# Hybrid pooling and state-space layer on one core: split weights of z, z' and v kept in HBM, output weights prepared earlier, last z blocks between the first steps

## The chip, the core and the metric

The kernel runs on one core of a Trainium2 chip. The metric is the device time of one execution in microseconds (us); less is better. The core has five engines with queues of their own: TensorE (PE, with its weight loads as PEld), VectorE (DVE), ScalarE (ACT), GpSimd (POOL) and SyncE (SP, which here only starts DMA transfers). ACT starts transfers as well.

## The reference

One layer over 2048 latent tokens of width 1024 with a prefix of 256 context tokens. A normed and modulated input hm is projected to five parts: v (1024, for a pooling mixer), z' (its gate), z (the gate of the state-space mixer), x, B and C (2048 in all) and dt. The pooling mixer takes box means of v over windows 2, 4, 8, 16 on a 32 x 64 grid, less v itself, through a linear map for each group. The state-space mixer is a chunked scan in both directions, started from the context's final states. Both branches meet in one output projection.

```
hm = rmsnorm(h, norm_w) * (1 + scale) + shift;  p = hm @ w_in
y_pool = pool_mixer(v, pool_w, pool_scale) * silu(z')
y_s    = rmsnorm_by_group(ssd_bidir(conv(x, B, C), dt) * silu(z)) * ssd_norm_w
h      = h + g * (concat[y_pool, y_s] @ w_out);  out = rmsnorm(h, final_norm_w)
```

g comes, like scale and shift, from silu(c) @ w_ada + b_ada.

## The kernel before, in words

Products with weights are made in two parts: a weight or a token value is rounded to a high part, and the rest is kept as a low part; a product is hi x hi + hi x lo + lo x hi, three matrix products (project, from L227). The function weights (raw_weights L212 and split_weights) reads 0.5 MB of raw weights on SP's queue into one of two "wraw" buffers of rpool, lets ACT copy the high part (L219) and GpSimd subtract for the low part (L220), into one of two "w" buffers of wpool (1 MB each). All of it is one function, hybrid_block. Outside tc.manual_schedule() a planner orders the instructions of each engine, by written order and the times at which it expects operands; inside, they stand as written. The stages, with the times at which they run:

- **Start** (0 to 160). The linear map of the pool is multiplied into the weights of v (pool_map) and written to s_wp (map_store, L375, on SP). The modulation is made from w_ada. Tokens, one object for each block of 512 tokens, loads the tokens (x, xs, x2; L152), makes the norm (squares, mean, spread) and the modulated block hm[b] in a big buffer ("slot", of which there are four). Block b = 0 is modulated while the norms of blocks 1 and 2 are made; after each block come the columns 0 and 1 of x, B, C.
- **x, B, C stage** (160 to 492). The loop over columns ct from 2 to 15: 128 columns of weights each, read and split one column ahead; the context's product (ct under 12), four blocks of 512 tokens, the convolution on ACT and DVE (conv, L270), and writes to s_xt, s_bt and s_bc (conv_store, L258 on SP). At ct 10 to 13 gate_row reads eight rows of w_ada for g, through rpool; DVE sums them in gacc, which is written to s_gate.
- **Sweep stage** (492 to 823). For each of eight column groups j, the products of z, z' and v for the upper half of the tokens (blocks 2 and 3), with weights(...) for each. Between them runs sweep, the backward scan over 18 chunks and 4 groups: first makes split operands (bt, L641; xw, L644; xh, L649; xr, L651), second the states. At j = 1 the sum over partitions of gacc is multiplied into two PSUM banks gb, which stay held until the last rescale. From j = 2 on, eight blocks of w_out are read through rpool, scaled by rescale (L725, on DVE, from PSUM) and written to s_wo (unsplit).
- **Box stage** (823 to 1057). The lower half of the tokens (blocks 0 and 1): for each j of order the products of v and z' (box_pair) with box means on DVE, results in zt (one buffer), written to s_yp by ACT's queue after L828; with the first four, the z groups 0 to 3. following() hands out the weights and starts those of the next product. With the last four, prepare(0) to prepare(3). Then z groups 4 and 5, 1057 to 1079.
- **First steps** (1057 to 1150), written by hand in the string RAMP. 64 steps (chunk c, group g) make the forward scan, the gated norm and the output projection. Step.load starts six transfers on SP (L880 to L889): bc from s_bc (with silu of z), e1 and e2, tk, st. The chain of the norm is squares, square_sum, norm_mm, norm1, norm2, diag (L1014), spread. outputs is L973 and L979. Between the steps stand the z groups 6 and 7 (z makes the product, zg the silu and the write to s_bc) and the preparation of w_out: prep_load, prep_scale (k under 8), prep_hi, prep_lo, each through rpool, into four big buffers wout, each of which takes over the slot of a token block or a box buffer (more). prepare(9) to prepare(15) come after RAMP.
- **Steady steps** (1150 to 1681), all as written in ORDER.

## Time and profile before

| | us |
|---|---|
| median of 3 runs | 1691.6 |
| runs, lowest to highest | 1691.33 to 1699.04 |
| the profiled execution | 1691.25 |
| its span, first to last instruction | 1689.5 |
| PE busy in it | 1626.3 (96%) |
| DVE busy in it | 1209.4 (72%) |

The profile is of one execution. The page gives busy times by engine, the transfers, and the chain of work that ended last; views of the trace give the same by stretch of time (windows), by line and form of instruction, as a list in order of time (timeline), and as waits: an engine's idle time put down to the work that ended it. PEclk is TensorE's granted clock as a share of full speed (1.00 is 2.4 GHz, 0.50 is 1.2 GHz). A DMA share is the mean busy share of 16 DMA engines. Times within the execution count from the span's start.

### The profile page before, as it was taken

To read this page: it belongs to the slowest core of one execution; us is meant where nothing else is said; L and a number is where in the kernel's file an instruction comes from. 1 tells how busy PE (TensorE), PEld (TensorE's weight loads), DVE (VectorE), ACT (ScalarE), POOL (GpSimd) and SP (SyncE) were. 2 spreads that over 40 slices of the span, in tenths; PEclk is the share of its full clock that TensorE was granted. 3 is DMA by queue.
4 is the path that set the end of the run, shared out by engine and by line. 5 is a ranking of instruction groups with operands and counts; after the bars stand their busy time and mean duration, and the time that the engine had idled before them with its cause. 6 is when DMAs were issued, how large, how long until landed. Compare 5 with 4: busy or idle time off the path is not lost. (4 is left out here: it accounts for less than half of the span.)

```text
span 1689.5 us, 25001 instructions
## 1 busy us (share of the span) xinstructions
PE 1626.3 (96%) x7786; PEld 1306.6 (77%) x7786; DVE 1209.4 (72%) x2514; ACT 768.4 (45%) x1841; POOL 599.5 (35%) x667
## 2 busy tenths in 40 slices
PE   8889999999999999999999989869999999999997
PEld 6668888888887887787887868757888888888886
DVE  2575755566772888886199998547788888888885
ACT  5563453433453444443212122455565556555653
POOL 1231111111223667775433334323333333333331
PEclk9989999999999999999999999989999999999999
DMA  9823333466564678878624356675666667666762
GB/s 388 283 75 100 76 74 73 93 155 155 144 137 153 203 248 252 255 249 272 207 87 150 114 184 187 188 223 184 186 194 208 195 203 199 198 208 192 194 194 83
DMA packets 315543, 302.57 MB, mean 179 GB/s; under 512 B 132626, under 2 KB 244114, under 8 KB 312851
## 3 DMA queue, kind: packets, MB, share of 16 engines
q1 hardware_dynamic: 246594, 237.27, 48.9%
q10 hardware_dynamic: 68816, 63.71, 11.3%
q8 instruction: 61, 1.00, 0.2%
q14 instruction: 72, 0.58, 0.1%
HBM read 207.28 MB, written 93.62 MB: 178 GB/s over the span
## 5 line engine op out<-in xcount | busy, mean ns | idle before, releaser
L52 PE MATMUL px<-hm,w_x 128*128 128x512 f32 x1536 | 364.8, 397 | 2.7 <-ACT hm L205 2.4
L52 PEld LDWEIGHTS px<-hm,w_x 128*128 128x128 f32 x1536 | 288.0, 188 | 73.3 <-ACT hm L205 4.1
L52 PE MATMUL po<-wout,yp 128*128 128x512 f32 x768 | 213.0, 413 | 0.0
L52 PE MATMUL po<-wout,ys 128*128 128x512 f32 x768 | 211.0, 410 | 0.0
L52 PE MATMUL pz<-hm,w_z 128*128 128x512 f32 x768 | 188.9, 398 | 0.7 <-POOL w_z L220 0.7
L270 DVE SCALAR_TENSOR_TENSOR cacc<-u,conv_w,cacc 128x512 f32<-128x512 f32 x168 | 141.5, 854 | 66.3 <-POOL u L320 47.5
L52 PEld LDWEIGHTS pz<-hm,w_z 128*128 128x128 f32 x768 | 145.0, 189 | 36.0 <-POOL w_z L220 1.1
L52 PEld LDWEIGHTS po<-wout,yp 128*128 128x128 f32 x768 | 135.9, 190 | 34.7 <-issue 10.6
L52 PEld LDWEIGHTS po<-wout,ys 128*128 128x128 f32 x768 | 136.3, 190 | 23.7
L960 POOL TENSOR_TENSOR yp<-yl,yp 128x256 fp32r<-128x256 f32 x64 | 50.3, 786 | 229.2 <-ACT yp L956 220.8
L644 DVE TENSOR_TENSOR xw<-xt,w_t 128x256 f32<-128x256 f32 x144 | 99.3, 728 | 31.5 <-POOL xr L651 17.0
L651 POOL TENSOR_TENSOR xr<-xw,xh 128x512 fp32r<-128x512 f32 x72 | 99.7, 1387 | 27.4 <-ACT xh L649 27.4
L960 POOL TENSOR_TENSOR ys<-yg,ys 128x256 fp32r<-128x256 f32 x64 | 63.1, 986 | 116.9 <-ACT ys L956 66.6
L52 PE MATMUL ivationFunctionType.Copy<-hm,ivationFunctionType.Copy 128*128 128x512 f32 x384 | 97.7, 401 | 2.3 <-POOL ivationFunctionType.Copy L220 1.7
L52 PE MATMUL pv<-hm,w_v 128*128 128x512 f32 x384 | 92.9, 402 | 5.9 <-ACT zt L795 5.9
L52 PE MATMUL ivationFunctionType.Silu<-hm,ivationFunctionType.Silu 128*128 128x512 f32 x384 | 95.9, 396 | 0.0
L649 ACT CAST xh<-xw 128x512 fp32r<-128x512 f32 x72 | 44.7, 621 | 110.0 <-DVE xw L644 48.9
L52 PE MATMUL pzp<-hm,w_q 128*128 128x512 f32 x384 | 91.3, 396 | 1.2 <-ACT va L788 1.2
L52 PEld LDWEIGHTS pv<-hm,w_v 128*128 128x128 f32 x384 | 73.6, 192 | 24.1 <-ACT zt L795 6.3
L52 PEld LDWEIGHTS ivationFunctionType.Copy<-hm,ivationFunctionType.Copy 128*128 128x128 f32 x384 | 73.1, 191 | 20.5 <-POOL ivationFunctionType.Copy L220 2.1
L52 PEld LDWEIGHTS pzp<-hm,w_q 128*128 128x128 f32 x384 | 72.0, 188 | 19.2 <-ACT va L788 1.6
L904 ACT ACTIVATE e<-e,nrb_t 128x128 f32<-128x128 f32 x256 | 81.1, 388 | 12.2 <-DMA e<-s_rows 11.9
(269 smaller groups left out, 3046.3 us busy)
## 6 DMA issues: line engine op xcount, KB each, us to landing
e<-s_rows SPq DMA_DIRECT2D x128, 256.0 KB, 5.1
s_tok<-tkw ACTq DMA_DIRECT2D x64, 256.0 KB, 3.0
bc<-s_bc SPq DMA_DIRECT2D x64, 256.0 KB, 4.3
st<-s_tok SPq DMA_DIRECT2D x64, 256.0 KB, 5.5
xt<-s_xt SPq DMA_DIRECT2D x72, 128.0 KB, 3.4
ada<-in_w_ada_dram SPq DMA_DIRECT2D x8, 1024.0 KB, 15.7
wraw_x<-in_w_xbc_dram SPq DMA_DIRECT2D x16, 512.0 KB, 4.4
s_bc<-cacc ACTq DMA_DIRECT2D x32, 256.0 KB, 3.2
```

Source lines behind the costliest of these rows:

```text
L52: nc.tensor.matmul(o, l, r, start=start, stop=stop)
L270: nc.vector.scalar_tensor_tensor(acc, u[:, k:k + n], conv_w[:, ct, k:k + 1], acc, op0=ALU.mult, op1=ALU.add)
L644: nc.vector.tensor_tensor(xw[:, s], h4(xt), w_t[:, s, c, 4 * g:4 * g + 4].unsqueeze(2).broadcast_to([P, 4, 64]), op=ALU.mult)
L649: nc.scalar.copy(xh, xw)
L651: nc.gpsimd.tensor_tensor(xr, xw, xh.bitcast(F32), op=ALU.subtract)
L904: nc.scalar.activation(s.e2[:, h, :], s.e2[:, h, :], AF.Identity, bias=nrb_t[:, s.c, 4 * s.g + h:4 * s.g + h + 1])
L960: nc.gpsimd.tensor_tensor(y[:, 1], src, y[:, 0].bitcast(F32), op=ALU.subtract)
```

## The change

Weights of z, z' and v: the sweep stage splits each group once (kept_weights) and writes both parts, 1 MB, to s_w on SP's queue, each after the read of the next group's raw weights (save). The box stage and the first steps read them back as split tiles (saved_weights), with no work on ACT or GpSimd. rpool closes after the sweep stage.

Output weights: prep(k) reads, scales, splits and writes all 16 blocks of w_out to s_wo, in columns 8 to 11 of the x, B, C stage, four a column, through rpool and one "wo" buffer. prepare(k) becomes one read of 1 MB. For this the gate rows move from columns 10 to 13 to columns 3 to 6, their product goes through two aux PSUM tiles back into gacc in SBUF, and s_gate and the banks gb are gone. The raw weights of columns 3 to 15 are read on ACT's queue instead of SP's.

z groups 4 and 5 of the lower half move into RAMP, among the first steps, with groups 6 and 7; the function w there takes the next weights. prepare(4) to prepare(13) stand in RAMP as reads, prepare(14) and (15) behind it.

Start: the buffer of block 1 is taken right after its read; the writes to s_wp, x2 and the reads of blocks 2 and 3 move into the modulation of block 0, the writes inside a block that orders what it holds behind the last square of block 1. Smaller moves: rowscale and allone are made before the x, B, C stage, wd lies in another pool, kp opens ahead of RAMP.

```diff
     s_wp = dram("s_wp", [8, P, 8, P])
+    s_w = dram("s_w", [24, P, 2, 8, P])
...
-    s_gate = dram("s_gate", [P, 1024])
-    s_wo = dram("s_wo", [8, P, 1024])
+    s_wo = dram("s_wo", [16, P, 2, 1024])
...
+    wpool = wstack.enter_context(tc.tile_pool(name="wpool", bufs=2, side="right"))
     rpool = rstack.enter_context(tc.tile_pool(name="rawp", bufs=2, side="right"))
-    wpool = wstack.enter_context(tc.tile_pool(name="wpool", bufs=2, side="right"))
...
     latent(1, xs[:, 1])
-    x2 = slot("x2", [P, 2, 8, 512], F32)
-    latent(2, x2[:, 0])
-    latent(3)
-    for g in range(4):
-        map_store(g)
+    latent_slot(1)
...
     for b in range(4):
-        if b > 0:
+        if b > 1:
             latent_slot(b)
...
+            if (b, k) == (0, 1):
+
+                with tc.issue_after(tok[1].last.ins):
+                    for g in range(4):
+                        map_store(g)
+                x2 = slot("x2", [P, 2, 8, 512], F32)
+                latent(2, x2[:, 0])
+                latent(3)
...
-            nc.scalar.dma_start(s_gate, gacc)
+            for j in range(2):
+                gb = aux(f"gb{j}")
+                mm(gb, allone, gacc[:, 512 * j:512 * j + 512], True, True)
+                nc.scalar.copy(gacc[:, 512 * j:512 * j + 512], gb)
+
+    def prep(k):
+
+        raw = rpool.tile([P, 1024], F32, tag="wraw", name=f"wos{k}")
+        nc.sync.dma_start(raw, d["w_out"][k * P:(k + 1) * P, :])
+        for j in range(2):
+            js = slice(512 * j, 512 * j + 512)
+            nc.vector.scalar_tensor_tensor(raw[:, js], raw[:, js], rowscale[:, k:k + 1], gacc[:, js],
+                                           op0=ALU.mult, op1=ALU.mult)
+            w = gp.tile([P, 2, 512], F32R, tag="wo", bufs=1, name=f"wo{k}_{j}")
+            nc.scalar.copy(w[:, 0], raw[:, js])
+            nc.gpsimd.tensor_tensor(w[:, 1], raw[:, js], w[:, 0].bitcast(F32), op=ALU.subtract)
+            nc.sync.dma_start(s_wo[k, :, :, js], w.bitcast(F32))
...
         if ct < 15:
-            wx[ct + 1] = weights(d["w_xbc"][ct + 1], f"x{ct + 1}")
+            raw = rpool.tile([P, 8, P], F32, tag="wraw", name=f"wraw_x{ct + 1}")
+            nc.scalar.dma_start(raw, d["w_xbc"][ct + 1])
+            wx[ct + 1] = split_weights(raw, f"x{ct + 1}")
...
             col.conv()
+            if 8 <= ct < 12:
+                prep(4 * ct - 32 + b)
...
-        if ct in (10, 11, 12, 13):
+        if 3 <= ct < 7:
             for k in range(2):
-                gate_row(2 * ct - 20 + k)
+                gate_row(2 * ct - 6 + k)
...
-        def rescale(raw, k):
-
-            for j in range(2):
-                js = raw[:, 512 * j:512 * j + 512]
-                nc.vector.scalar_tensor_tensor(js, js, rowscale[:, k:k + 1], gb[j], op0=ALU.mult, op1=ALU.mult)
+        unsaved = []
+
+        def kept_weights(i, src, nm):
+
+            w = weights(src, nm)
+            save()
+            unsaved.append((i, w))
+            return w
+
+        def save():
+            for i, w in unsaved:
+                nc.sync.dma_start(s_w[i], w.bitcast(F32))
+            unsaved.clear()
...
-            w = weights(d["w_z"][j], f"z{j}_2")
+            w = kept_weights(j, d["w_z"][j], f"z{j}_2")
...
-            if j == 1:
-                gacc = rpool.tile([P, 1024], F32, tag="wraw", name="gacc2")
-                nc.sync.dma_start(gacc, s_gate)
-                gb = [pp(f"gb{j}") for j in range(2)]
-                for j in range(2):
-                    mm(gb[j], allone, gacc[:, 512 * j:512 * j + 512], True, True)
-            for k in {1: (), 7: (5, 6, 7)}.get(j, (j - 2,) if j else ()):
-                raw = rpool.tile([P, 1024], F32, tag="wraw", name=f"wos{k}")
-                nc.sync.dma_start(raw, d["w_out"][1024 + k * P:1152 + k * P, :])
-                rescale(raw, 8 + k)
-                nc.scalar.dma_start(s_wo[k], raw)
...
-                w = weights(src, f"p{j}_{fn}")
+                w = kept_weights((8 if fn == AF.Silu else 16) + j, src, f"p{j}_{fn}")
...
+        save()
+    rstack.close()
...
+    def saved_weights(i, nm):
+        w = wpool.tile([P, 2, 8, P], F32R, tag="w", name=f"w_{nm}")
+        nc.sync.dma_start(w.bitcast(F32), s_w[i])
+        return w
...
-            ahead.append(weights(*sources.pop(0)))
+            ahead.append(saved_weights(*sources.pop(0)))
...
     def prepare(k):
-        prep_load(k)
-        prep_scale(k)
-        prep_hi(k)
-        prep_lo(k)
+        nc.sync.dma_start(wout[k // 4][:, k % 4].bitcast(F32), s_wo[k])
...
-    for i in (4, 5):
-        w = following()
-        for b in lower:
-            z_block(ep, w, i, b)
-        if i == 4:
-            prepare(i)
     estack.close()
     yp_ = ctx.enter_context(tc.tile_pool(name="poolp", bufs=2))
-    ws = [following() for _ in range(2)]
+    ws = []
...
     def z(j, b):
-        zps[j, b] = z_product(ws[j - 6], j, b)
+        zps[j, b] = z_product(ws[j - 4], j, b)
...
+    def w():
+        ws.append(following())
+
+    kp = ctx.enter_context(tc.tile_pool(name="workp", bufs=2))
...
     RAMP = """
-    0:load prep_load/5 1:load 0:scores 0:carried 0:shift 0:mask 0:exponents prep_scale/5 1:shift 0:steps_mix
-    prep_hi/5 logs 0:decay z/6/0 1:scores 1:carried zg/6/0 z/7/0 0:mix 0:from_states prep_load/6 
...
+    0:load w z/4/0 1:load 0:scores 0:carried 0:shift 0:mask 0:exponents 0:steps_mix logs 0:decay
+    w z/5/0 0:mix 0:from_states 0:mix2 prepare/4 prepare/5 1:scores 1:carried 1:shift 1:mask 1:exponents 1:steps_mix
+    1:decay zg/4/0 zg/5/0 2:load 0:load_pool 0:outputs z/4/1 1:mix 1:from_states 1:mix2 0:gate logs 0:squares
+    0:square_sum 0:state 0:norm_mm 1:outputs 2:scores 2:shift 2:mask 2:exponents 2:steps_mix 2:decay z/5/1
+    0:norm1 1:gate 0:norm2/0 0:norm2/1 0:norm2/2 0:norm2/3 0:diag 1:squares 1:square_sum 1:load_pool prepare/6
+    prepare/7 0:spread 2:carried zg/4/1 zg/5/1 w 0:scale z/6/0 w 2:mix 2:from_states 2:mix2 logs 0:ssd_hi 0:ssd_lo
+    1:norm_mm 2:outputs 1:norm1 1:state 1:norm2/0 1:norm2/1 1:norm2/2 1:norm2/3 1:diag z/7/0 2:gate 2:squares
+    2:square_sum 1:spread zg/6/0 zg/7/0 more 3:load prepare/8 prepare/9 1:scale logs 0:pool_hi 0:pool_lo 1:ssd_hi
+    1:ssd_lo prepare/10 prepare/11 z/6/1 2:norm_mm 3:scores 3:carried 3:shift 3:mask 3:exponents 3:steps_mix 3:decay
...
     """
...
-    for k in range(9, 16):
+    for k in range(14, 16):
         prepare(k)
-    rstack.close()
+    wstack.close()
```

## Rows read from the trace of the kernel before

**Rows 1.** The page, busy time of each engine, its share of the span and instructions.

```profile
PE 1626.3 (96%) x7786; PEld 1306.6 (77%) x7786; DVE 1209.4 (72%) x2514; ACT 768.4 (45%) x1841; POOL 599.5 (35%) x667
```

**Rows 2.** Windows by stage: stretch, length, busy of PE PEld DVE ACT POOL, PEclk, DMA, GB/s.

```profile
0.00:160.00 160.00, 139.29 (x662) 107.12 (x663) 81.76 (x149) 83.56 (x170) 38.76 (x48) 0.95 0.62 221
160.00:492.00 332.00, 332.00 (x1532) 272.42 (x1531) 219.94 (x308) 146.35 (x224) 54.31 (x146) 1.00 0.51 110
492.00:823.00 331.00, 325.04 (x1372) 258.76 (x1371) 230.67 (x383) 136.19 (x295) 202.11 (x163) 0.99 0.72 229
823.00:1057.00 234.00, 226.95 (x963) 181.87 (x962) 196.40 (x72) 46.58 (x65) 85.57 (x54) 0.99 0.47 148
1057.00:1150.00 93.00, 72.43 (x326) 56.67 (x324) 51.99 (x108) 46.77 (x94) 31.35 (x22) 0.89 0.67 202
1150.00:1690.00 540.00, 530.63 (x2938) 429.71 (x2938) 428.65 (x1498) 308.92 (x996) 187.37 (x234) 1.00 0.64 188
```

**Rows 3.** Waits of PE: us in total, times, longest us.

```profile
PE n L52 <- ACT dg L1014: 8.9, 2, 4.9
...
PE yo L52 <- DMA st<-s_tok: 6.8, 1, 6.8
PE rstd_l L52 <- ACT dgl L134: 6.1, 2, 5.9
PE pv L52 <- ACT zt L795: 5.9, 1, 5.9
PE st L52 <- DVE bt L641: 3.4, 4, 1.8
```

**Rows 4.** Timeline of SP's queue, 45 to 62: start, us, what.

```profile
49.79 1.55 SPq L152 DMA_DIRECT2D x<-in_xT_dram  x1
...
56.13 5.56 SPq L152 DMA_DIRECT2D xs<-in_xT_dram  x1
```

**Rows 5.** Groups by line and form, L651 and L649: busy, mean ns.

```profile
L651 POOL TENSOR_TENSOR xr<-xw,xh 128x512 fp32r<-128x512 f32 x72 | 99.7, 1387 | 27.4 <-ACT xh L649 27.4
...
L649 ACT CAST xh<-xw 128x512 fp32r<-128x512 f32 x72 | 44.7, 621 | 110.0 <-DVE xw L644 48.9
```

**Rows 6.** Timelines of DVE (1078 to 1095) and of POOL (270 to 284).

```profile
1079.99 1.13 DVE L899 SCALAR_TENSOR_TENSOR e<-e,af_t,e 128x128 f32<-128x128 f32 x4
1081.38 1.41 DVE L725 SCALAR_TENSOR_TENSOR wor<-wor,rowscale,gb 128x512 f32<-128x512 f32 x2 [0.26 <-DMA wor<-in_w_out_dram]
1086.38 6.12 DVE L935 SCALAR_TENSOR_TENSOR m<-cbl,dt_t,m 128x128 f32<-128x128 f32 x4 [3.59 <-ACT m L927]
...
277.53 2.42 POOL L220 TENSOR_TENSOR w_x<-wraw_x,w_x 128x1024 fp32r<-128x1024 f32 x1 [0.77 <-ACT w_x L219]
```

**Rows 7.** DMA issues: count, KB each, median us from issue to landing.

```profile
wraw_x<-in_w_xbc_dram SPq DMA_DIRECT2D x16, 512.0 KB, 4.4
...
s_wo<-wos ACTq DMA_DIRECT2D x8, 512.0 KB, 3.2
```

**Rows 8.** Timeline of PE, columns 11 to 15 and both ends of the boxes.

```profile
379.66 112.15 PE L52 MATMUL px<-hm,w_x 128*128 128x512 f32 x480
...
823.11 11.36 PE L52 MATMUL pz<-hm,w_z 128*128 128x512 f32 x48
...
1056.77 22.56 PE L52 MATMUL pz<-hm,w_z 128*128 128x512 f32 x96
```

**Rows 9.** Timeline of SP's queue, 310 to 340.

```profile
318.97 15.00 SPq L258 DMA_DIRECT2D s_bt<-u  x12
```

**Rows 10.** A window of 10 us in the sweep stage, columns of rows 2.

```profile
700.00:710.00 10.00, 10.00 (x44) 8.08 (x44) 10.00 (x13) 3.84 (x12) 8.72 (x7) 1.00 0.80 261
```

**Rows 11.** The chain that ended last, 1040 to 1165: start, us, what.

```profile
1065.17 5.09 DMA s_yp<-zt
...
1071.24 7.30 DMA e<-s_rows
```

**Rows 12.** A window of 5 us in the first steps, columns of rows 2.

```profile
1125.00:1130.00 5.00, 3.16 (x17) 2.50 (x17) 2.82 (x7) 2.42 (x4) 0.00 (x0) 0.50 0.84 216
```

More of the change, by code (lines that the diff above doesn't have):

```diff
@@ L333, in hybrid_block @@
     dt_raw = const("dt_raw", [P, NC2, 32], pool=dp)
-    wd = dp.tile([P, 8, P], F32R, tag="wd", name="wd")
+    wd = sp.tile([P, 8, P], F32R, tag="wd", bufs=1, name="wd")
     ctxt = Tokens(hc, 256, d["ctxT"], 1, "c", wpool.tile([P, 8, 256], F32, tag="w", name="xc"))
@@ L763, in hybrid_block @@
         if i < 4:
-            sources.append((d["w_z"][i], f"z{i}"))
-        sources += [(s_wp[j], f"v{j}"), (d["w_zp"][j], f"q{j}")]
-    sources += [(d["w_z"][i], f"z{i}") for i in range(4, 8)]
-    ahead = [weights(*sources.pop(0))]
+            sources.append((i, f"z{i}"))
+        sources += [(16 + j, f"v{j}"), (8 + j, f"q{j}")]
+    sources += [(i, f"z{i}") for i in range(4, 8)]
+    def saved_weights(i, nm):
+        w = wpool.tile([P, 2, 8, P], F32R, tag="w", name=f"w_{nm}")
+        nc.sync.dma_start(w.bitcast(F32), s_w[i])
+        return w
+    ahead = [saved_weights(*sources.pop(0))]
     def following():
@@ L833, in hybrid_block @@
     wout = [slot("wout0", [P, 4, 2, 1024], F32R)]
-    raws = {}
-    def prep_load(k):
-        raws[k] = rpool.tile([P, 1024], F32, tag="wraw", name=f"wor{k}")
-        nc.sync.dma_start(raws[k], s_wo[k - 8] if k >= 8 else d["w_out"][k * P:(k + 1) * P, :])
-    def prep_scale(k):
-        if k < 8:
-            rescale(raws[k], k)
-    def prep_hi(k):
-        nc.scalar.copy(wout[k // 4][:, k % 4, 0, :], raws[k])
-    def prep_lo(k, eng=None):
-        wo = wout[k // 4][:, k % 4]
-        eng = eng or (nc.gpsimd if k in (1,3,4,5,7,13,15) else nc.vector)
-        eng.tensor_tensor(wo[:, 1, :], raws[k], wo[:, 0, :].bitcast(F32), op=ALU.subtract)
     def prepare(k):
-        prep_load(k)
-        prep_scale(k)
-        prep_hi(k)
-        prep_lo(k)
+        nc.sync.dma_start(wout[k // 4][:, k % 4].bitcast(F32), s_wo[k])
     with tc.tile_pool(name="boxp", bufs=1) as xp:
@@ L1203, in hybrid_block @@
-    other = {f.__name__: f for f in (prep_load, prep_scale, prep_hi, prep_lo, z, zg, logs, work, more)}
+    other = {f.__name__: f for f in (prepare, z, zg, logs, w, more)}
     RAMP = """
-    0:load prep_load/5 1:load 0:scores 0:carried 0:shift 0:mask 0:exponents prep_scale/5 1:shift 0:steps_mix
-    prep_hi/5 logs 0:decay z/6/0 1:scores 1:carried zg/6/0 z/7/0 0:mix 0:from_states prep_load/6
-    0:mix2 1:mask 1:exponents 2:load prep_scale/6 1:steps_mix prep_hi/6 1:decay zg/7/0 2:scores 2:carried more
@@ L1211, in hybrid_block @@
-    1:from_states 1:mix 0:outputs z/6/1 prep_lo/5 prep_load/7 0:load_pool prep_lo/6
-    0:gate 2:mask prep_scale/7 1:mix2 prep_load/8 1:load_pool 0:squares 2:shift
-    2:steps_mix 0:square_sum 2:exponents 1:outputs 0:norm_mm z/7/1 more work prep_hi/8 prep_hi/7 zg/6/1 prep_lo/8
-    0:state prep_lo/7 3:load 2:from_states 1:gate 0:pool_hi 1:squares zg/7/1 logs 0:norm1
-    1:square_sum 0:norm2/0 1:pool_hi 2:decay 2:mix 0:pool_lo 1:pool_lo 3:scores 1:norm_mm 0:out/0/0
-    0:out/0/1 1:norm1 0:norm2/1 0:norm2/2 0:norm2/3 0:diag 0:spread 2:mix2 3:mask 2:outputs 1:out/0/0 0:scale 3:carried 1:out/0/1
@@ L1219, in hybrid_block @@
+    2:norm1 2:state z/7/1 1:pool_hi 1:pool_lo zg/6/1 zg/7/1 more prepare/12 prepare/13 logs 2:norm2/0 2:norm2/1
+    2:norm2/2 2:norm2/3 0:out/0/0 0:out/0/1 1:out/0/0 1:out/0/1
     """
```

13 lines of the change are left out of this document (3 added, 10 removed).

## The prediction, made before the changed kernel was run

> **What bounds the kernel now.** I read the busy table first [rows 1]: TensorE is busy 1626.3 of 1689.5 us, so an edit can only win back TensorE's idle time, 63 us, and the time in which its clock is down. The profiled execution took 1691.25 us, 1.75 more than its span and 0.35 under the median of the three runs, 1691.6; the sum is made against 1691.25. Next I read the span by stage [rows 2], the stage's length less its PE column. The x, B, C stage (160 to 492) has no TensorE idle at all. The rest is 20.7 us in the start, 6.0 in the sweep stage (492 to 823), 7.1 in the box stage (823 to 1057), 20.6 in the first steps (1057 to 1150) and 9 in all that follows. The waits of TensorE [rows 3] name them: the spread of the second token block's norm in the start (6.1), the DVE's split bt in the sweep (3.4), ACT's silu into zt in the box stage (5.9), and in the first steps the chain of the step norm (8.9) and one load of st (6.8). About 0.5% (8.5 us) is what a measurement of this kernel can tell from no change.
>
> **The start.** The read of the third block (x) goes out before that of the second (xs), at 49.8 against 56.1, and writes of s_wp stand around both [rows 4]. After the change block 1 gets its own buffer without waiting for the s_wp writes, and x and s_wp come later. The read at 56.1 could then go out some 5 us earlier, behind the first row of writes instead of the second. What that buys is the wait for the spread, 6.1 us [rows 3], and perhaps 2 us of the clock behind it (the stage's mean is 0.95, [rows 2]); x, now late, is first needed after a whole block of products. I take -5, between 0 and -8. The block that ties the stores to an instruction of ACT holds only transfers that SP starts, so it may tie nothing; then only the written order acts, and I leave the 5.
>
> **The x, B, C stage.** Added: 16 preparations of output weights, each a read of 0.5 MB, two DVE scalings, two ACT copies, two GpSimd subtractions, two writes of 0.5 MB; and the two gate products, moved from the sweep, which are worth nothing in the sum. Of engine time there is enough: GpSimd is at 54.3 of 332 us and would add 32 x 1.39 = 44; ACT 146 + 32 x 0.62 = 166 [rows 2, 5]; DVE 220 + 32 x 0.7 = 243 [rows 2, 6]. DVE does lose time when GpSimd subtracts: four small operations that take 1.13 us in one row took 6.12 beside two subtractions [rows 6]; if all 44 us were lost so, DVE would stand at 287 of 332, still under. What is short is buffers. The split piece wo has one buffer, so a half goes copy 0.62, subtract 1.39, write 3.2 [rows 5, 7], then the next: 5.2 us, and 32 halves take 167. The preparations share the two raw buffers with the x weights, and behind the raw weights of a column that wait for their turn stands TensorE. In this sum I let the x weights, now read on ACT's own queue, get a buffer ahead of the preparations that were written earlier, so that the chain simply fills the time from column 8 to the stage's end, 191 us (column 8 begins at 301, three columns of 22.4 and 2.9 of context ahead of column 11, whose latent products begin at 379.7 [rows 8]), and I charge +4 for a late column, between 0 and the +44 of the first rival. The SP queue is crossed too: a row of twelve s_bt writes held it for 15 us [rows 9], and the s_wo writes go behind such a row.
>
> **The sweep.** Removed: 16 scalings on DVE (16 x 0.7 = 11 us; three blocks of weights stood at the end, where bt is waited for), eight reads and eight writes of 0.5 MB, and the two PSUM banks that the gate product held from here to the first steps. Added: 24 writes of 1 MB on SP. They wait for a split that has ended by then, because each is written behind the next weights' read; behind them on SP stand the sweep's reads of xt and bl and its writes of hb. Added less removed is 24 - 8 = 16 MB in 331 us, 48 GB/s. The stage runs at 229 GB/s and a share of 0.72 [rows 2]; at 0.80 it moved 261 [rows 10], so 277 would be a share of about 0.85: close, not full. I take -2 (of the 3.4 on bt), between -4 and +10 (a few reads of 3 to 5 us stuck behind writes). The Trainium skill, DMA: Bandwidth & Descriptors, section Bandwidth, gives 425 GB/s for a 16 MB transfer; by that figure an estimate of the stage would have a third to spare and no cost at all. The trace's share leaves less room than that.
>
> **The box stage.** Removed: 20 splits of weights on ACT and GpSimd and four preparations. Added: weight reads of 1 MB in place of 0.5, and only two weight tiles in place of two raw and two split ones; a read starts when the tile before last is free and then has a group's 11.2 us, against some 5, the 5.09 of a 1 MB write [rows 11]. Twenty groups of 11.2 us make 224 us, yet the stage takes 1056.77 - 823.11 = 233.7 [rows 8]: 9.7 us are lost, 5.9 of them through the full PSUM behind zt [rows 3], the rest in the clock after it and in a small wait. The two banks given back alone let TensorE run on for two blocks while silu waits, and DVE loses the 8 scalings and the collisions with GpSimd. I take -9, between 0 and -9.7.
>
> **The first steps.** Eight z blocks (8 x 5.6 = 45 us of products) now stand between the steps, four of them, 22.6 us, moved in from before [rows 8]. They can cover the norm's waits. Against this: the first load of a step came just behind the write of the last box result, a write of 5.09 us that ended at 1070.3; e of that load went out at 1071.2 [rows 11]. Those four blocks covered that wait; now one block of 5.6 does. The last box group would end at 1047; silu, one DVE product and the write bring the first load to about 1056, its scores to 1060, its states to 1064: TensorE idles some 9 us. Then 3 MB (z6 and two output tiles) stand on SP ahead of the third step's load, and the fourth load waits until z6 and z7 are written: 0 to 9 and 4 to 8 us. Lost before: 20.6 us idle and some 5 of half clock (0.50, TensorE's lower level of 1.2 GHz, in a stretch of this stage) [rows 2, 12]. Lost after: 9 + 3 + 5 and about 2 of clock, 19 in round numbers. I take -7; bounds -20 (nearly all gone) and +9 (every wait at its worst). The 12 preparations on ACT, DVE and GpSimd that go away free these engines, not TensorE.
>
> **The sum.** -5 + 4 - 2 - 9 - 7 = -19: 1691.25 - 19 = 1672.
>
> **Rivals.** First, slower: the raw buffers go out in written order. Column 13's weights are then behind preparation 15 and need what preparation 14 frees. The first preparation can begin when column 8's split ends at 280 [rows 6] plus a read of 4.4 [rows 7]; 29 halves of 5.2 later it is 435; then 2 to the end of its subtraction, 4.4 to read, and 3.6 to split the weights (2.42 for GpSimd's part and twice 0.62 for ACT's) [rows 5, 6]: 445. Column 13 begins at 379.7 + 2 x 22.4 = 424.5 (five columns in 112.15, [rows 8]). TensorE stands 21 us; with each write delayed by 0.8 on the SP queue (halves of 6.0) it is 44. At 35, and without the +4, the kernel takes 1691.25 - 23 + 35 = 1703. It decides from a half of about 4.5 us on. For it: the single wo buffer, and the measured 3.2 us of a write. Against it: the reads have moved to ACT's queue and stand in no row of SP's any more. The Trainium skill, DMA: Bandwidth & Descriptors, section Issuing engines are not separate DMA queues, says that starting transfers from several engines saves only the starter's time; by that rule the move shortens no read, and this rival's 1703 would come out. No row here shows a read of weights from ACT's queue.
>
> Second, no change: the first steps give back what the box stage won. The load that waits for the result, the third and the fourth load each at their upper bound make 9 + 9 + 8 us and the clock 4 after them, 30 in place of 26; with a sweep that gains nothing, because the writes fill its DMA engines, and a start whose order doesn't change: 1691.25 + 4 + 0 - 9 + 4 = about 1690. For it: the e of the first load took 7.3 us to land [rows 11]. Against it: eight blocks leave much to put between.
>
> Third, the change doesn't act at the start: -14 in place of -19, 1677, still faster, so it is inside the forecast's own range, 1657 to 1682.
>
> **How the numbers follow.** Forecast and its variants 0.47, first rival 0.31 (of it 0.27 beyond +0.5% and 0.04 within), second 0.18, and 0.04 for a loss through the sweep's writes that reaches the size of the first rival. So faster 0.47, same 0.04 + 0.18 = 0.22, slower 0.27 + 0.04 = 0.31. The range takes in the forecast's lower side (1657) and reaches into the first rival to 1709; what lies above (halves of 6 us and more) and below is under 2 in 10.
>
> **What would show it.** Right: no TensorE wait on the x weights between 400 and 470, a box stage of 225 us with no wait on zt, the norm's waits gone from the first steps, the first steps' loss under 20 us, a busy total still at 1626. Wrong: a wait of TensorE on ACT's or GpSimd's part of w_x of 10 us or more (first rival); waits on bc or st of 10 us and more after 1047 (second); DMA shares of 1.0 in the sweep with waits on bt or xr.

## The result, and the profile after

The changed kernel takes 1779.38 us (median of 4 runs, 1775.73 to 1780.92) where the kernel before took 1691.46 beside it: a ratio of 1.052, 95% interval 1.0494 to 1.0545. The forecast was 1672, with a range up to 1709. The profiled execution took 1775.73 us.

The page of the changed kernel, span and busy times (before: [rows 1]):

```profile
span 1773.8 us, 25046 instructions
PE 1638.1 (92%) x7786; PEld 1310.6 (74%) x7786; DVE 1159.6 (65%) x2505; ACT 754.8 (43%) x1839; POOL 540.9 (30%) x668
```

TensorE's work is what it was but for 12 us of slower clock, and its idle time went from 63 to 136 us. The same stages as in [rows 2], in windows of the changed kernel; the columns are those of [rows 2], the bounds are where the same products begin:

```profile
0.00:150.70 150.70, 129.40 (x624) 99.30 (x625) 73.21 (x138) 78.59 (x163) 38.55 (x47) 0.95 0.65 234
150.70:551.90 401.20, 349.58 (x1572) 285.11 (x1571) 244.92 (x343) 165.99 (x259) 97.49 (x177) 0.93 0.61 153
551.90:898.50 346.60, 328.20 (x1370) 256.95 (x1369) 228.98 (x374) 139.34 (x299) 200.64 (x164) 0.99 0.80 265
898.50:1124.70 226.20, 224.37 (x962) 180.39 (x961) 154.79 (x63) 23.80 (x40) 7.12 (x32) 1.00 0.61 206
1124.70:1245.00 120.30, 86.28 (x382) 67.51 (x382) 35.89 (x118) 43.71 (x101) 13.89 (x19) 0.83 0.71 247
```

The x, B, C stage, which had no idle at all, now has 51.6 us of it; the sweep 18; the boxes 2; the first steps 34. In the x, B, C stage the products also run 9 us longer than before, at a granted clock of 0.93 where it was 1.00. The waits of TensorE in the changed kernel say on what (before: [rows 3]):

```profile
PE px L52 <- ACT w_x L219: 42.9, 2, 22.0
PE yo L52 <- DMA st<-s_tok: 18.2, 3, 9.8
PE st L52 <- DVE bt L665: 15.4, 17, 2.3
PE cb L52 <- DMA bc<-s_bc: 14.5, 2, 9.2
PE pc L52 <- ACT w_x L219: 8.7, 1, 8.7
...
PE rstd_l L52 <- ACT dgl L134: 5.8, 1, 5.8
```

All runs are read by the same four lengths: when the first z product begins (the end of the x stage), the sweep (to the first z product of the lower half), the boxes (to the end of the last z' product) and the rest. Spans are of the profiled executions; ratios are to the kernel before on the same chip.

| run | first z at | sweep | boxes | rest | span | ratio (interval) |
|---|---|---|---|---|---|---|
| before | 491.7 | 331.5 | 233.8 | 632.6 | 1689.5 | 1 |
| after | 551.9 | 346.5 | 226.2 | 649.1 | 1773.8 | 1.052 (1.0494 to 1.0545) |
| e2_two_small | 533.9 | 344.9 | 226.6 | 650.2 | 1755.6 | 1.0407 (1.0386 to 1.0428) |
| e3_x_on_sp | 545.0 | 340.9 | 226.5 | 649.5 | 1761.9 | 1.0466 (1.0436 to 1.0496) |
| e4_spread | 510.9 | 354.1 | 226.2 | 647.5 | 1738.6 | 1.0297 (1.0275 to 1.0318) |
| e5_few_saves | 552.8 | 324.4 | 226.6 | 649.8 | 1753.6 | 1.039 (1.0371 to 1.0408) |
| e6_saves_act | 551.9 | 336.3 | 228.1 | 647.9 | 1764.3 | 1.0451 (1.0413 to 1.0488) |
| e7_old_ramp | 552.2 | 345.2 | 226.3 | 626.3 | 1750.0 | 1.0384 (1.0347 to 1.0422) |
| e8_load_first | 552.6 | 345.8 | 226.6 | 648.5 | 1773.5 | 1.0505 (1.0472 to 1.0537) |
| e9_one_prep | 494.1 | 345.1 | 228.2 | 649.9 | 1717.3 | 1.0145 (1.0106 to 1.0184) |
| e10_no_keep | 494.9 | 318.4 | 226.3 | 633.6 | 1673.1 | 0.9899 (0.9884 to 0.9914) |
| e11_all_mended | 503.3 | 348.1 | 226.6 | 631.5 | 1709.5 | 1.0148 (1.0126 to 1.017) |
| e12_hold_banks | 494.6 | 318.4 | 226.5 | 632.8 | 1672.3 | 0.99 (0.9873 to 0.9927) |
| e13_keep_alone | 493.7 | 349.8 | 224.2 | 625.7 | 1693.3 | 1.0027 (1.001 to 1.0043) |
| e14_hold_longer | 494.0 | 318.4 | 232.6 | 627.5 | 1672.5 | 0.9912 (0.9896 to 0.9929) |
| e15_keep_four | 493.7 | 318.9 | 229.9 | 627.0 | 1669.5 | 0.989 (0.9875 to 0.9905) |

From before to after the span grew by 84.3: the start -0.6, the x stage +60.9, the sweep +15.1, the boxes -7.6, the rest +16.5.

### The profile page after: what moved, and what is told of

It is laid out like the page before. It is cut to its first block, busy times and chain, and to the rows that moved or that the text cites. A ratio compares the mean times of both kernels' runs of the same rounds, so it can differ in the third digit from the quotient of the medians.

```text
span 1773.8 us, 25046 instructions
## 1 busy us (share of the span) xinstructions
PE 1638.1 (92%) x7786; PEld 1310.6 (74%) x7786; DVE 1159.6 (65%) x2505; ACT 754.8 (43%) x1839; POOL 540.9 (30%) x668
## 4 chain that ended last, share of the span: by engine, by line
PE 51%; DMA 15%; DVE 5%; issue 3%; POOL 2%; SPq 1%; ACT 1%; ACTq 0%; DVEq 0%; POOLq 0%
PE po L52 21%; PE pz L52 6%; PE pzp L52 5%; PE pv L52 4%; DMA s_wo<-wo 3%; DMA xt<-s_xt 3%; PE yo L52 3%; PE y L981 2%; PE ivationFunctionType.Silu L52 2%; PE y L987 2%; PE ivationFunctionType.Copy L52 2%; DMA s_tok<-hb 2%; DVE xw L668 2%; DVE cacc L270 1%; PE n L52 1%
## 5 line engine op out<-in xcount | busy, mean ns | idle before, releaser
L52 PE MATMUL px<-hm,w_x 128*128 128x512 f32 x1536 | 371.5, 401 | 45.7 <-ACT w_x L219 42.9
L52 PEld LDWEIGHTS px<-hm,w_x 128*128 128x128 f32 x1536 | 292.0, 191 | 118.3 <-ACT w_x L219 43.8
L52 PE MATMUL pz<-hm,w_z 128*128 128x512 f32 x768 | 194.4, 404 | 1.5 <-DMA w_z<-s_w 1.3
L668 DVE TENSOR_TENSOR xw<-xt,w_t 128x256 f32<-128x256 f32 x144 | 104.7, 768 | 70.3 <-DMA xt<-s_xt 50.7
L675 POOL TENSOR_TENSOR xr<-xw,xh 128x512 fp32r<-128x512 f32 x72 | 99.1, 1378 | 71.9 <-ACT xh L673 51.6
L52 PE MATMUL ivationFunctionType.Silu<-hm,ivationFunctionType.Silu 128*128 128x512 f32 x384 | 100.0, 405 | 2.5 <-POOL ivationFunctionType.Silu L220 2.2
L52 PEld LDWEIGHTS ivationFunctionType.Silu<-hm,ivationFunctionType.Silu 128*128 128x128 f32 x384 | 74.1, 193 | 21.1 <-POOL ivationFunctionType.Silu L220 2.7
L907 DVE SCALAR_TENSOR_TENSOR e<-e,af_t,e 128x128 f32<-128x128 f32 x256 | 72.7, 344 | 20.9 <-ACT e L912 20.9
## 6 DMA issues: line engine op xcount, KB each, us to landing
wout<-s_wo SPq DMA_DIRECT2D x16, 1024.0 KB, 10.1
```

What stands on the lines that cost most here:

```text
L52: nc.tensor.matmul(o, l, r, start=start, stop=stop)
L668: nc.vector.tensor_tensor(xw[:, s], h4(xt), w_t[:, s, c, 4 * g:4 * g + 4].unsqueeze(2).broadcast_to([P, 4, 64]), op=ALU.mult)
L675: nc.gpsimd.tensor_tensor(xr, xw, xh.bitcast(F32), op=ALU.subtract)
L907: nc.vector.scalar_tensor_tensor(s.e1[:, h, :], s.e1[:, h, :], af_t[:, 0, s.c, i:i + 1], s.e2[:, h, :], op0=ALU.subtract, op1=ALU.min)
```

## The experiments

### The x, B, C stage

TensorE's timeline of the changed kernel at columns 11 to 13 (start, length, what; in brackets the idle time ahead of it and what ended it):

```profile
386.79 0.80 PE L52 MATMUL pc<-hc,w_x 128*128 128x256 f32 x2 [8.70 <-ACT w_x L219]
...
436.75 24.18 PE L52 MATMUL px<-hm,w_x 128*128 128x512 f32 x96 [21.95 <-ACT w_x L219]
481.90 70.19 PE L52 MATMUL px<-hm,w_x 128*128 128x512 f32 x288 [20.97 <-ACT w_x L219]
```

The releaser is the split of the columns' weights. What was late ahead of it is in the chain of the changed kernel that ended last, here from 440 to 447 (start, us, what); the same four pieces come again and again up to 487, at times with others between:

```profile
440.26 0.63 ACT wo L595
440.90 0.07 issue
440.96 1.31 POOL wo L596
442.29 3.58 DMA s_wo<-wo
445.97 0.63 ACT wo L595
```

Undisturbed, a half takes 5.7 us here, from copy to copy, and 5.1 the next time; the 32 halves of the tile wo, in this view of the changed kernel (engine, operation, count, shortest, median and longest ns, first and last start), take 284.4 to 485.4, 201 us for 31 steps, 6.5 each:

```profile
L595 ACT CAST wo<-wos x32: 605/620/624, 284.4 to 485.4; 128x512 fp32r<-128x512 f32 x32
L596 POOL TENSOR_TENSOR wo<-wos,wo x32: 1262/1292/1689, 285.1 to 486.1; 128x512 fp32r<-128x512 f32 x32
```

How this chain holds the x weights is seen on ACT's queue ahead of column 13 (timeline of ACT in the changed kernel):

```profile
474.46 0.37 ACTq L608 DMA_DIRECT2D wraw_x<-in_w_xbc_dram  x1
480.28 0.62 ACT L595 CAST wo<-wos 128x512 fp32r<-128x512 f32 x1 [7.19 <-DMA s_wo<-wo]
480.81 1.04 ACT L219 CAST w_x<-wraw_x 128x1024 fp32r<-128x1024 f32 x1
```

GpSimd's subtraction of a half ends at 474.4, a raw buffer comes free, and at 474.46 the read of the weights goes out. The copy that makes their high part then stands in ACT's row behind the copy of a half, which waits for the write of the half before; TensorE goes on at 481.90.

Four runs parted the causes. **e2_two_small**: quarters, two buffers.

```diff
+            for q in range(2):
+                qs = slice(512 * j + 256 * q, 512 * j + 256 * q + 256)
+                w = gp.tile([P, 2, 256], F32R, tag="wo", bufs=2, name=f"wo{k}_{j}_{q}")
...
+                nc.sync.dma_start(s_wo[k, :, :, qs], w.bitcast(F32))
```

> The output weights are split in quarters of 256 columns through two buffers of half the size (the same memory). Theory A (the chain copy, subtract, write through the one wo buffer sets the pace, and the x weights wait in the shared raw buffers behind it): the chain needs some 4 us for a half in place of 5 to 6, all preparations are done before column 13 would begin, TensorE's wait on w_x falls from 51 to under 5 us, the z products begin near 495 in place of 552, total 1720 to 1727. Theory B (the reads of x weights go out late because they stand on ACT's queue): nothing changes, 1779. Theory C (DVE and GpSimd get in each other's way): more and smaller instructions, 1779 or more.

The first z product came at 533.9, 18 us earlier, not 57; TensorE's wait fell from 51.6 to 34.3. The direction is A's, the size is not: the 64 quarters still took 285.9 to 465.6, 2.9 a quarter and 5.7 a half. The write of a quarter took 2.9 us where that of a half took 3.6, but this alone doesn't make 5.7: copy, subtraction and write of a quarter are 0.41 + 0.74 + 2.9 = 4.0 us, and two buffers would allow a half in that time, as A reckoned. In the chain that ended last the writes of s_wo are 62.7% from 430 to 490 in the changed kernel and 24.0% from 380 to 470 in e2; reads of w_out (11.7%), writes to s_bt (9.0%) and many short pieces on DVE, GpSimd and SP's queue stand in their place. The single buffer is one part of the cost; what share each of the others has was not tried.

**e3_x_on_sp**: the queue of the x weights' reads.

```diff
-            nc.scalar.dma_start(raw, d["w_xbc"][ct + 1])
+            nc.sync.dma_start(raw, d["w_xbc"][ct + 1])
```

> The reads of x weights go back to SP's queue, all else as in the changed kernel. Theory A: the buffer decides, not the queue, so 1779 within 5. Theory B: the wait on w_x goes, 1725.

It won 12 us in the median and 9 by the ratios, 7 of them in this stage: more than A allowed, a small part of what B asked. TensorE's wait on w_x is 46.7 us in place of 51.6: ACT's queue makes the reads somewhat later, the buffers make them late. Why the sweep is 5.6 us shorter as well is not shown.

**e4_spread**: the same work, other columns.

```diff
-            if 8 <= ct < 12:
-                prep(4 * ct - 32 + b)
+            if 7 <= ct < 15 and b % 2:
+                prep(2 * ct - 14 + b // 2)
```

> Two preparations a column in columns 7 to 14 in place of four in 8 to 11; the same buffers and instructions. Theory A: a column's weights stand behind two preparations, four halves of 5 to 6 us, 20 to 24 in a column of 22.4 to 25.3, so the chain about keeps pace: z products begin between 495 and 510, total 1722 to 1737. Theory B: 1779 (the wait is on ACT's queue, whatever the spread). Theory C: 1779 (the same colliding work).

The wait on w_x is gone altogether, and B and C with it. What TensorE still waits for in this stage of e4 is ACT's emptying of PSUM and, at its end, the first z weights:

```profile
PE px L52 <- ACT u L315: 9.5, 7, 3.0
PE pz L52 <- ACT w_z L219: 2.4, 1, 2.4
```

The stage still ends 19 us later than before, and the sweep is 7.6 longer than in the changed kernel, with 20.2 us of waits on bt in place of 15.4. The total (1740.53) stands just above what A gave.

**e9_one_prep**: one preparation.

```diff
-            if 8 <= ct < 12:
-                prep(4 * ct - 32 + b)
+            if (ct, b) == (8, 0):
+                prep(0)
...
-        nc.sync.dma_start(wout[k // 4][:, k % 4].bitcast(F32), s_wo[k])
+        nc.sync.dma_start(wout[k // 4][:, k % 4].bitcast(F32), s_wo[0])
```

> One output weight block is prepared in place of 16 (column 8, first block), and every output tile is read from it, so the output projection uses block 0 throughout; what is left out is 15 preparations. Theory A (the preparations' chain holds the x weights' buffers): no wait on w_x of more than 3 us, first z product at 492 to 496 in place of 552, total 1716 to 1724. Rival G (the gate rows in columns 3 to 6, or the reads on ACT's queue, cost a part of the 60): first z product after 500, total above 1727.

No wait of TensorE is left in the stage, the first z product begins at 494.1, and the kernel takes 1716.52. So 58 of the stage's 61 us are the 15 preparations; the moved gate rows, and the reads on ACT's queue with no preparations beside them, cost under 3.

### The sweep

**e5_few_saves** writes 3 of 24 groups.

```diff
-                nc.sync.dma_start(s_w[i], w.bitcast(F32))
+                if i % 8 == 0:
+                    nc.sync.dma_start(s_w[i], w.bitcast(F32))
...
-        nc.sync.dma_start(w.bitcast(F32), s_w[i])
+        nc.sync.dma_start(w.bitcast(F32), s_w[i // 8 * 8])
```

> Only 3 of the 24 writes of split weights are made (those of j = 0) and read back for every j, so the box stage and the first steps use the first group's weights throughout; what is left out is 21 MB of writes. Theory W (the writes delay the sweep's reads, by SP's order or by the DMA engines): the sweep stage falls from 346.5 us to about 331, TensorE's wait on bt from 15.4 to 4 or less, total 1764. Rival P (another order that the planner chose, or late convolutions pushed into the sweep by the late x stage): 346 and 1779.

324.4, under the 331 of W: the 21 writes left out had cost 22 us, and what the change removed from the stage had won some 7. The window of the sweep in e5 (columns of [rows 2]):

```profile
552.84:877.22 324.38, 321.37 (x1369) 258.56 (x1368) 231.97 (x374) 140.12 (x299) 199.19 (x164) 0.99 0.68 216
```

The share is 0.68 here and 0.80 with the writes; no wait on bt is left. **e6_saves_act** changes only the queue of the writes (nc.scalar in place of nc.sync in save).

> The 24 writes of split weights start from ACT's queue in place of SP's. Theory Q (what costs in the sweep is the place that the writes take in SP's row, ahead of the reads of xt): the sweep stage falls from 346.5 to 325 to 331 us, as with the writes left out (324.4), TensorE's wait on bt from 15 to under 4, total 1757 to 1764. Theory D (the 24 MB themselves make the other transfers late, whichever queue starts them): the sweep stays at 340 to 350 and the total at 1773 to 1782.

336.3, between Q and D: 10 of the 22 us go with the place in SP's row, 12 stay. TensorE's wait on bt went from 15.4 to 6.6.

Whether these 12 are the bytes or the writes' new place in ACT's row, the run doesn't part, but the traces say more. TensorE waits for DVE's bt, and DVE for the reads of xt (waits of DVE in the sweep, before and in the changed kernel):

```profile
DVE xw L644 <- DMA xt<-s_xt: 10.9, 4, 4.1
...
DVE xw L668 <- DMA xt<-s_xt: 50.7, 19, 6.3
```

The two longest of the 19 waits, as windows of the changed kernel (columns of [rows 2]; the DMA share is the last but one):

```profile
793.75:800.10 6.35, 6.35 (x29) 5.03 (x27) 0.00 (x1) 1.19 (x3) 1.92 (x2) 1.00 0.88 298
823.75:829.46 5.71, 5.71 (x26) 4.63 (x25) 0.01 (x1) 1.11 (x3) 1.49 (x2) 1.00 0.97 322
```

Over all of these waits longer than 0.3 us the share is 0.96 on the mean, against 0.80 for the stage; it is 0.94 over those of e6, which still come to 27.6 us, and 0.77 before. Of the 69 stretches of 5 us in the changed sweep 18 stand at 0.95 or more, in e5 5 of 64. So the DMA engines were full, or nearly, where DVE waited, and the mean over the stage hid it. That speaks for the bytes as the cause of most of the 12 us.

### The first steps

SP's queue of the changed kernel at the third step's load (start, us, what):

```profile
1159.02 0.32 SPq L793 DMA_DIRECT2D w_z<-s_w  x1
1159.43 0.85 SPq L865 DMA_DIRECT2D wout<-s_wo  x2
1160.39 0.55 SPq L888 DMA_DIRECT2D bc<-s_bc  x1
```

The read of z6's weights waits for the end of z4's second product (1159.0), two output tiles go out behind it, and only then bc, which TensorE gets at 1169.77 after 9.24 us of idle.

**e7_old_ramp** puts z groups 4 and 5 ahead of the steps again and takes the hand-written order of before:

```diff
+    for i in (4, 5):
+        w = following()
+        for b in lower:
+            z_block(ep, w, i, b)
+        if i == 4:
+            prepare(i)
...
+    ws = [following() for _ in range(2)]
...
+    0:load prepare/5 1:load 0:scores 0:carried 0:shift 0:mask 0:exponents 1:shift 0:steps_mix
+    logs 0:decay z/6/0 1:scores 1:carried zg/6/0 z/7/0 0:mix 0:from_states prepare/6 
...
```

> The z groups 4 and 5 stand ahead of the first steps again and the steps follow the hand-written order of before, with the preparations as reads of 1 MB; all else as changed. Theory R (the order of the changed first steps makes the waits: the loads stand behind the result's write, behind weight reads and behind the z groups that they need): from the end of the boxes to the end of the kernel 649 falls to 625 to 635, total 1757 to 1766. Rival S (the reads of 1 MB themselves fill the queue, 16 MB in place of 8, in any order): 642 or more, total 1772 or more.

626.3 in place of 649.1, as R has it: the new order costs 23. It is also 6 us less than before. That the ready output tiles won these is not shown: e13, below, keeps the weights of z but still splits the output weights among the first steps, and has 625.7.

**e8_load_first** moves one read of weights and two of output tiles behind the load:

```diff
+    def r():
+        ahead.append(saved_weights(*sources.pop(0)))
...
-    w z/5/0 0:mix 0:from_states 0:mix2 prepare/4 prepare/5 1:scores 1:carried 1:shift 1:mask 1:exponents 1:steps_mix
-    1:decay zg/4/0 zg/5/0 2:load 0:load_pool 0:outputs z/4/1 1:mix 1:from_states 1:mix2 0:gate logs 0:squares
+    w z/5/0 0:mix 0:from_states 0:mix2 1:scores 1:carried 1:shift 1:mask 1:exponents 1:steps_mix
+    1:decay zg/4/0 zg/5/0 2:load r prepare/4 prepare/5 0:load_pool 0:outputs z/4/1 1:mix 1:from_states 1:mix2 0:gate logs 0:squares
...
-    prepare/7 0:spread 2:carried zg/4/1 zg/5/1 w 0:scale z/6/0 w 2:mix 2:from_states 2:mix2 logs 0:ssd_hi 0:ssd_lo
+    prepare/7 0:spread 2:carried zg/4/1 zg/5/1 r w 0:scale z/6/0 w 2:mix 2:from_states 2:mix2 logs 0:ssd_hi 0:ssd_lo
...
```

> In the changed first steps the read of z6's weights and of output tiles 4 and 5 stand behind the load of step 2 on SP's queue in place of ahead of it; all else as changed. Theory R: the wait of 9.2 us on bc of step 2 falls to 0 to 4, and from the boxes' end to the kernel's end it is 640 to 644 in place of 649, total 1770 to 1774. Rival Z (step 2 waits for its own input, the z groups 4 and 5 that were moved in, and would wait as long in any row of SP): the wait stays above 7 us, total 1776 to 1782.

The wait went, the time did not. TensorE's timeline of e8 has it elsewhere:

```profile
1161.89 0.46 PE L52 MATMUL cb<-bc 128*128 128x128 f32 x2 [0.94 <-DMA bc<-s_bc]
1170.72 0.69 PE L52 MATMUL n<-dg,allone 128*128 128x128 f32 x2 [2.78 <-ACT dg L1025]
1184.99 7.18 PE L52 MATMUL pz<-hm,w_z 128*128 128x512 f32 x24 [4.29 <-DMA w_z<-s_w]
```

9.24 us on bc became 0.94, and 2.78 on the norm and 4.29 on z7's weights took its place. R's mechanism is right, its price as a single edit was not: the queue holds too much for this order, whichever piece is put first.

### What the change's parts are worth on a sound base

**e10_no_keep** is the kernel before with the gate rows in columns 3 to 6 and all 16 blocks scaled, unsplit, two a column:

```diff
+    def prep(k):
+
+        raw = rpool.tile([P, 1024], F32, tag="wraw", name=f"wos{k}")
+        nc.sync.dma_start(raw, d["w_out"][k * P:(k + 1) * P, :])
+        nc.vector.scalar_tensor_tensor(raw, raw, rowscale[:, k:k + 1], gacc, op0=ALU.mult, op1=ALU.mult)
+        nc.sync.dma_start(s_wo[k], raw)
...
+            if 7 <= ct < 15 and b % 2:
+                prep(2 * ct - 14 + b // 2)
...
-        if ct in (10, 11, 12, 13):
+        if 3 <= ct < 7:
...
```

> The kernel before with a part of the change alone: the gate rows and their product in columns 3 to 6 (no PSUM banks held), all 16 output weight blocks scaled, not split, in columns 7 to 14, two a column; weights of z, z' and v split twice as before, first steps in the order of before without the scalings. Theory K (what the box stage won, 7.6 us, comes from the two PSUM banks and the scalings that are gone, and the sweep wins 7 without scalings where no writes stand against it): the sweep 324 to 327, the boxes 224 to 228, the rest 628 to 632, the x stage to 496, total 1673 to 1682. Rival L (the box stage's gain comes from the splits that are gone): the boxes stay at 232 to 234, total 1680 to 1689. Rival M (preparations in the x stage cost, even unsplit, because of the shared raw buffers): first z product after 500, total above 1686.

It is 1% faster than the kernel before: 1673.77 against 1690.84. Its x stage ends at 494.9 with 16 preparations in the columns of e4, which took until 510.9; e10 leaves out their copies, subtractions and half of the written bytes (and reads the x weights on SP's queue). Its sweep has no TensorE idle left and is shorter than the 324 to 327 of K, and its boxes are as short as in the changed kernel with all 20 splits still in them (windows of e10, the sweep and the boxes):

```profile
494.90:813.28 318.38, 318.38 (x1369) 256.85 (x1368) 229.24 (x369) 138.34 (x296) 201.55 (x165) 1.00 0.66 211
813.28:1039.54 226.26, 224.96 (x962) 180.25 (x961) 191.27 (x63) 46.22 (x64) 91.58 (x54) 1.00 0.48 150
```

L and M are out. **e13_keep_alone** adds the kept weights to e10 (kept_weights and save, saved_weights, as in the change) and nothing else.

> The kernel of e10 with the split weights of z, z' and v kept in HBM as in the change (24 writes of 1 MB on SP's queue in the sweep, 24 reads of 1 MB for the lower half), and nothing else of the change added. Theory: keeping them is a loss by itself, the writes cost the sweep some 20 us and the boxes gain nothing, as TensorE doesn't wait for splits there: sweep 338 to 346, boxes 225 to 228, total 1692 to 1703. Rival: the reads relieve ACT, GpSimd and DVE in the boxes and first steps and give back half or more: total under 1685.

The same two windows of e13:

```profile
493.65:843.48 349.83, 327.79 (x1370) 257.12 (x1368) 229.53 (x374) 139.44 (x299) 199.48 (x164) 0.99 0.80 264
843.48:1067.64 224.16, 224.16 (x962) 180.49 (x961) 157.27 (x65) 27.77 (x44) 11.99 (x34) 1.00 0.59 197
```

Against e10 the sweep loses 31.4 us, the boxes win 2.1, the rest wins 7.9: 20 us lost by the part that names the change. The sweep is longer than the 346 of the theory, and where the rival asked for half or more back, a third came. DVE is relieved of 34 us in the boxes (191.27 to 157.27), and TensorE, the bound, has 2.1 of it.

**e12_hold_banks** and **e14_hold_longer** were to part the freed PSUM banks from the scalings; both add to e10

```diff
+                gb = [pp(f"gb{i}") for i in range(2)]
+                for i in range(2):
+                    mm(gb[i][:, 0:P], allone, triU, True, True)
```

at j = 1 and read gb after the boxes, e14 together with bx[:, 0:1].

> The kernel of e10 with two PSUM banks of the products' kind held from the sweep (j = 1) to the end of the boxes, as the gate product held them before; two small products and two copies of one column are added, nothing else. Theory K1 (the two banks are what the boxes and the sweep won): the wait on ACT's zt of some 6 us is back, the boxes 232 to 234 us, the sweep 322 to 331, total 1681 to 1692. Rival K2 (the scalings on DVE that are gone won it): boxes 226 to 228, sweep 318, total 1674 to 1677.

e12 changed nothing, and couldn't: the planner moved the reading copies to 541 us, next to the products.

> As e12, whose two banks came free again 0.6 us after they were taken (the copies ran at 541 us), so that it tested nothing: now the reading operation takes a result of the box sums as well, and the banks are held from the sweep (j = 1) into the seventh of eight boxes. Theory K1 (the two banks): sweep 322 to 331, boxes 230 to 234 with a wait on ACT's zt, total 1680 to 1690. Rival K2 (the scalings): sweep 318 to 320, boxes 226 to 228, total 1672 to 1677.

In e14 the read came at 1022, and the boxes took 232.6 with the wait of before (waits of TensorE in e14's boxes):

```profile
PE pv L52 <- ACT zt L793: 4.6, 1, 4.6
PE pzp L52 <- ACT va L786: 1.2, 1, 1.2
```

So the boxes' gain is the banks', as K1 said; but the sweep kept its 318.4, which K1 had not, and the total is e10's within the intervals, because the rest is 6 us shorter. The first load goes out at 1053.9 in both: it waits for the last box result, whose product begins on DVE at 1046.4 in e10 and 1045.9 in e14. From there on e10's lead shrinks, from 5.5 us at the end of the boxes to 1.4 when the third step's st is used (windows between the two points, e10 and e14):

```profile
1039.54:1085.22 45.68, 38.62 (x161) 30.16 (x160) 22.05 (x28) 21.01 (x35) 13.90 (x7) 0.94 0.69 202
1045.01:1086.63 41.62, 36.42 (x161) 29.29 (x159) 16.20 (x26) 21.11 (x35) 14.74 (x7) 0.99 0.74 212
```

TensorE idles 7.1 us in e10 and 5.2 in e14, and its granted clock is 0.94 and 0.99. What the banks win in the boxes is given back in the first steps, as idle time and as clock.

**e15_keep_four** keeps z 4 to 7 alone, on e10.

> The kernel of e10 with only four groups kept split, z 4 to 7, whose lower half is multiplied last: 4 writes of 1 MB in the sweep in place of 24, 4 reads. From e13 (all 24: sweep +31, boxes -2, first steps -8 against e10). Theory: the first steps' 8 us come from z 6 and 7, whose splits stand between the steps, and a sixth of the writes costs 5 or less: sweep 318 to 324, the rest 626 to 630, total 1668 to 1674. Rival: they come from elsewhere, the rest stays at 632 to 634, total 1674 to 1680.

The rest is 627.0, 6.6 less than e10's, the sweep pays 0.5 and the boxes 3.6. By e14 a later end of the boxes comes off the rest, so some 3 of the 6.6 are won, and that they come from z 6 and 7 is not shown. At 1671.11 it is the lowest median of all, but its interval and e10's overlap.

**e11_all_mended** is the changed kernel with e2, e3, e4, e6 and e7 together.

> The changed kernel with every mend at once: preparations spread two a column over columns 7 to 14, in quarters through two small buffers, x weights read on SP's queue, writes of split weights on ACT's queue, the order of before in the first steps. If the losses of the stages are separate, as the theories A, Q and D, and R have it, they add: first z product at 496 to 508, the sweep 335 to 345, the boxes 226 to 229, the rest 626, total 1687 to 1710. If one loss only moves into the next stage (late convolutions into the sweep, late writes into the boxes), the total is above 1715.

1714.95, between the sum and what the other case asked: the x stage and the boxes came out as the sum has it, the sweep (348.1 where e6 had 336.3) and the rest (631.5 in place of 626) didn't. DVE's work in the sweep is 243.6 us there against 235.9 in e6: convolutions pushed out of the x stage by the preparations run in it, the last at 531.4, and between them TensorE waits 5.43 us, until 521.95, for ACT's split of weights. That part of the loss moves on; it is read from the trace and was not tried by itself.

## Why the prediction was wrong

- **What bounds.** Right: TensorE's idle time and clock are all that changed. DVE's, ACT's and GpSimd's busy times all fell and the kernel is slower.
- **The start**, -5 forecast, -0.6 measured. The read of xs goes out at 53.45 in place of 56.13 [rows 4], 2.7 us earlier and not 5: six of the eight s_wp writes still stood ahead of it, 11.64 us long. The block that was to tie them tied nothing, which the prediction had allowed for; the wait on the spread fell from 6.1 to 5.8.
- **The x, B, C stage**, +4 forecast, +60.9 measured. This is the step that failed: "In this sum I let the x weights, now read on ACT's own queue, get a buffer ahead of the preparations that were written earlier". They did not. The rival's mechanism held, with columns 11, 12 and 13 standing (8.7, 22.0, 21.0): a raw buffer comes free for the x weights only when a preparation lets go of it. Its price was low, because a half took 6.5 us in place of 5.2 to 6.0: the write took 3.6 in place of 3.2, and ACT's copy of a half, in its queue, waits for the buffer with all else of ACT behind it. With 6.5 the rival's own sum gives 284.4 + 29 x 6.5 + 10 - 424.5 = 58 us, where it took 35; measured are 51.6 of idle and 9 of slower clock, a term that it didn't have. By the Trainium skill, DMA: Bandwidth & Descriptors, section Issuing engines are not separate DMA queues, moving the reads shortens none; e3 agrees as to their length (4.4 us to landing in the median on either queue), though their place in a queue was worth 7 us of this stage there.
- **The sweep**, -2 forecast, +15.1 measured, outside the bounds of -4 to +10. The removed part was worth more than thought (7 in e5, 13 in e10); which piece of it was not parted, but e14 rules out the banks. The failed term is the added one: "close, not full" at a share of 0.85 read as no cost. The bytes came as worked out (0.80 and 265 GB/s over a longer stage), and the writes cost 22 to 31 us (e5, e13). A mean over the stage was the wrong thing to read: DVE's waits on the short reads of xt went from 10.9 to 50.7 us, and during them the share was 0.96. By e6 some 10 us of the cost are the place in SP's row; that most of the other 12 are the bytes is argued from the shares, not shown by a run of its own.
- **The boxes**, -9 forecast, -7.6 measured, by the mechanism forecast (e14), but the term should not have stood in the sum: e14 shows that it is given back in the first steps, where the first load waits for the last box result.
- **The first steps**, -7 forecast, +16.5 measured, beyond the bound of +9. The waits that were named all came: 5.30 and 3.87 us on the first load (9 forecast), 9.24 on the third, 4.46 on the fourth. Left out was the fifth load, 9.85, behind eight output tiles (10.1 us to landing in the median); and the third load's wait was taken at 3 in a range up to 9.
- **The range.** Each rival was given the forecast's values in the other stages, and the chances were dealt out as if only one could hold. The first rival, the second and the loss by writes all came at once, each in a stage of its own, and the stages' losses add.

## What to carry to other kernels

A step moved into a stage without idle time of the bounding engine must be costed by the buffer it shares with that engine's operands, not by the busy shares of the engines that do it: a chain through one buffer, measured from first to last, against the time until the next operand needs the same pool. Work that comes off engines beside the bound (here 20 splits) is worth nothing until a wait of the bounding engine names it; the bytes that pay for it are not free. Their room must be read where the engine waits, in stretches as short as the wait: a stage at a mean DMA share of 0.80 stood at 0.96 during the waits that cost it. And where stages end in a common wait, a gain ahead of the wait is no gain: look for what the next stage's first load waits for.

## What the runs showed of the hardware

Two vector operations of one form, in the boxes of e10 (with GpSimd's splits beside them) and of e13 (without), by line and form: out<-in, shapes, count, busy, mean ns:

```profile
L815 DVE TENSOR_TENSOR bx<-bx 128x2048 f32<-128x2048 f32 x8 | 26.5, 3315 | 0.4
```

```profile
L837 DVE TENSOR_TENSOR bx<-bx 128x2048 f32<-128x2048 f32 x8 | 18.3, 2292 | 0.4
```

The means are 3315 and 2292 ns. The Trainium skill, SBUF — State Buffer, section Who interferes with whom, says that a DVE instruction with two SBUF inputs contends with a GpSimd instruction that reads SBUF; the two rows agree with it. The mean hides which of the two pays. Three lines of e10's timeline:

```profile
977.54 2.29 DVE L820 TENSOR_TENSOR bx<-bx 128x2048 f32<-128x2048 f32 x1
977.65 4.44 POOL L219 TENSOR_TENSOR w_q<-wraw_q,w_q 128x1024 fp32r<-128x1024 f32 x1 [7.00 <-ACT w_q L218]
979.87 4.38 DVE L821 TENSOR_TENSOR bx<-bx,va 128x2048 f32<-128x2048 f32 x1
```

DVE's operation began 0.11 us ahead of the subtraction and took its 2.29 us, and the subtraction took 4.44, where one that met nothing took 2.40 (at 815.09); DVE's next began while the subtraction ran, and took 4.38. Here the later of two waited for the earlier. Not expected was the price of size in transfers: DMA issues of the changed kernel (KB each, median us to landing) show

```profile
s_wo<-wo SPq DMA_DIRECT2D x32, 512.0 KB, 3.6
...
wout<-s_wo SPq DMA_DIRECT2D x16, 1024.0 KB, 10.1
```

and the write of 256 KB in e2 took 2.9: half the bytes saved a fifth of the time. The reads of 1 MB into wout, sent out two or four at a time, took twice the 5.09 of a single write of that size [rows 11], where the reads of split weights, also 1 MB but sent out one at a time, took 5.2 to 5.4 in the median in the same kernel.
